# Prescribing TensorE's order in two expert loops, with the scatter and the gather cut in halves

## The chip, the cores and the metric

The kernel runs on one core of one Trainium2 chip. Its time is the device time in microseconds (us) of one launch. TensorE (PE) multiplies matrices and writes to PSUM; VectorE (DVE), ScalarE (ACT) and GpSimd (POOL) do the rest; SyncE (SP) only issues the loads of the weights. Each engine works off its own instructions strictly in the order in which they stand, so an instruction that has to wait holds up all behind it on that engine.

## The reference

Two layers over 256 tokens of 1024 channels, each a mixer and then an expert layer. Layer 0 mixes by attention and a recurrence, layer 1 by a Fourier transform. The expert layer is the same in both: a router picks two of sixteen experts for each token, and each expert is a gated product.

```
h2 = modulate(rmsnorm(x), shift2, scale2)
gates = top-2 of 16 experts per token, inside the best of 4 groups
for e in range(16):
    y = (silu(h2 @ w_gate[e]) * (h2 @ w_up[e])) @ w_down[e]     # 1024 -> 512 -> 1024, float32
    out = out + gates[..., e] * y
x = x + gate2 * out
```

## The kernel before

**Tiling.** Each expert has a list of up to 64 tokens. Two experts make a pair, one in the lower and one in the upper 64 columns of TensorE, and there are 8 pairs (p = 0 to 7) in a layer. Each pair does, in `up` and `down`: 16 matmuls `g` and 16 matmuls `u` (L1045; 8 channel chunks times 2 experts, alternating), the transposes `st` of the pair's one-hot rows (L1054), the activation `act` on ACT and DVE (L1050, L1051), the transposes `at` of `act` (L1064), the copy `aT` on DVE (L1066), and 16 matmuls `dn` in two column halves (L1079), whose results ACT and DVE bring out as `yH` and `yL` (L1081, L1082).

**Around the pairs.** `scatter` (L1018) adds a pair's `yH` and `yL` to the token rows: 8 matmuls `ya` with the one-hot matrix `ST`. It is called one pair later. `gather` (L977) builds the rows of four experts, that is of two pairs: a one-hot matrix `S` on DVE, and 32 matmuls `xg`, brought out of PSUM in eight pieces by ACT and DVE. It is called in the odd pairs 1, 3 and 5 for the two pairs that follow. `st` and `at` share one PSUM bank (`gps`); `g`, `u`, `xg`, `dn` and the final `z` share three (`wps`). Ahead of pair 2 stands `overflow`, a branch that all engines take past code that is not run here; before it `gate_rows` makes two matmuls `gb` (L428) and two copies on ACT (L429).

**The end.** In layer 1 the last pair goes to the output directly: `dn` in four pieces of 256 columns, and after each the four matmuls `z` (L1032) that spread it over the tokens. `up(7)` is called before `down(6)` there.

**The weights.** They run through 16 buffers of 1 MiB in one fixed order (`Stream`, L94); SP issues a load when the buffer's last reader is done. A pair needs 12 MiB.

**What sets the order.** The calls above only give each instruction a place in the program. Which instruction each engine gets next is decided, when the kernel is built, by a scheduler that plays the program through with modelled durations and takes what it believes ready. So instructions of `scatter` and `gather` may end up between those of `g`, `u` and `dn`.

Of the kernel before, what the change touches and what calls it, by code (L numbers as in the profile page):

```python
# [23 lines left out]
# weight buffers, each half a chunk  # L24
NSLOT = 16
# priority of splitting weights, and how far the modulation products stand back
PRI = 50
LOW = 60
# modulation chunks (layer, chunk) in the order they are worked off; those of ON_PE go to the tensor engine
ADA = [(0, 4), (0, 5), (0, 6), (0, 7), (0, 8), (0, 9), (1, 0), (1, 2), (1, 1), (1, 3), (1, 6)]  # L30
ON_PE = (2, 3, 9)
# chunks done in the waits of the expert layers, and beside the Fourier mixer
# [3 lines left out]
# load order of the mixer: modulation chunk (a), attention biases (B), projections Q, G, V, output rows o and p  # L36
ORDER = 'aaQBaaGaaaVpoaaaa'
# engine that takes the low part of each weight piece in K, Q, G, V and the two output products: vector or GpSimd
# [6 lines left out]
# steps of other work put between the steps of a product: modulation, then gates, scan, convolution or attention  # L45
# [6 lines left out]
# columns of the down projection, and of its last pair  # L52
# [4 lines left out]
class Chunk:  # L57
    """A [K * 128, f] piece of weights in two buffers: its first and second rows, or (by_cols) columns."""
# [26 lines left out]
    def used(self, k):  # L85
        """The k-th rows have had their last use."""
        if (k + 1) % self.n == 0:
            self.done(k // self.n)
# [5 lines left out]
class Stream:  # L94
    """Weights run through a fixed set of buffers, loaded in one order as buffers come free."""
# [13 lines left out]
    def add(self, items):  # L109
        """Items: a chunk; (chunk, half) or (chunk, half, columns) for a piece of it; or the (out, in) of another load."""  # L110
        for it in items:
            self.items.extend([(it, 0), (it, 1)] if isinstance(it, Chunk) else [it])
# [34 lines left out]
def hybrid_layers(  # L147
# [73 lines left out]
    def exp_items(l):  # L221
        order = [(n, p) for p in range(NE // 2) for n in "gud"]
        if l == 1:
            order[-6:] = [(n, p) for ns in ("gu", "d") for p in (6, 7) for n in ns]
        r = []
        for n, p in order:
            pair = [st.chunk((n, l, e), {"g": moe_g, "u": moe_u, "d": moe_d}[n][l, e], n == "d")
                    for e in (2 * p, 2 * p + 1)]
            if (l, n, p) == (1, "d", 7):
                # the last weights arrive in small pieces, so that the end of the work keeps up with them  # L230
                r += [(c, a // 512, slice(a % 512, a % 512 + b - a)) for a, b in zip(CUTS, CUTS[1:]) for c in pair]
            else:
                r += [(c, i) for i in range(2) for c in pair]
        return r
# [21 lines left out]
    # the first sections come in pieces, so that the first projection can start on the first channels  # L256
# [65 lines left out]
    def table(f, dep):  # L322
        """Have the activation table of f loaded ahead of its use, once dep is there."""
        return ac.activation(junk, dep, f, scale=0.0, bias=eps)

    def ada_te(l, parts, with_ctx=False, ps_=gps, after=None, used=None):
        """[1024, 128] pieces of the modulation product on the tensor engine; parts: (weights, column, section column).
        Returns the last step, which adds the bias."""
# [30 lines left out]
    def ada_step(l, j):  # L359
        """ada_pe as a task."""  # L360
        while not st.get(("a", l, j)).ready(1):
            yield
        finish = ada_pe(l, j)
        yield
        finish()
        yield

    def ada_ve(l, j):
        """One [1024, 512] piece of the modulation product: scaled rows summed lane by lane, then over the lanes."""
# [22 lines left out]
    def split(dst_h, src, dst_l, eng):  # L392
        """src = dst_h + dst_l exactly, both in float32r's precision."""
# [3 lines left out]
    def split_w(W, eng=gp):  # L397
        """A [128, 512] piece of weights in its two parts."""
# [6 lines left out]
    def mm3(p, lhs, rhs, start, stop):  # L405
        """p += lhs^T rhs from the split operands (high, low)."""
# [4 lines left out]
    def scale_col(name, mod, o, gain, s=slice(0, 8)):  # L411
        """gain * (1 + scale), per channel."""
# [6 lines left out]
    def gate_rows(l, o):  # L419
        """Broadcast a gate section (a column per channel chunk) over all partitions: [128, 1024]."""  # L420
# [11 lines left out]
    def rms_scale(src, dst, tb):  # L432
        """dst[:, tb] = src[:, tb] / rms over the channels."""
# [8 lines left out]
    class Task:  # L442
        """Work emitted step by step between the steps of other work."""
# [43 lines left out]
    # ==== layer 0: mixer ====  # L487
# [30 lines left out]
    def rows(p, w, nt, k):  # L518
        """p[t] += h[tokens of tile t] @ W[chunk k]"""
# [4 lines left out]
    def channels(p, w, n, k):  # L524
        """p[b] += (h[first n tokens] @ W[chunk k])^T, b a block of 128 channels; blocks that share a bank
        make one group, which its first matmul opens and its last one closes."""
# [5 lines left out]
    # x branch of the recurrence, transposed: [channels, latent | context]  # L532
# [19 lines left out]
    # freed buffers: attention biases with the recurrence's gate weights, keys, and queries with the output gate  # L552
# [30 lines left out]
    # depthwise convolution  # L583
# [19 lines left out]
    def gemm(W, step, on):  # L603
        """Eight steps over the contraction, the weights split two steps ahead, on the engines named by on."""
# [16 lines left out]
    def head_norm(ps_, dstT, gain):  # L621
        """QK-norm of [128 tokens, 8 heads x 64] tiles, transposed into dstT."""
# [24 lines left out]
    class Recurrence:  # L647
        """One direction of the gated linear recurrence over [channels, latent | context]."""
# [106 lines left out]
    # neighbourhood + context attention  # L755
# [36 lines left out]
    def weighted(h):  # L792
        """Heads h and h + 1, side by side on the tensor engine."""
# [27 lines left out]
    def add_gated(p, gate, tb, c, eng=ve):  # L821
        """x[columns c] += gate * p"""
# [5 lines left out]
    def project(srcH, srcL, W, order, on):  # L828
        """src^T @ W in four accumulators (token tile, half), src [128, 8, 256] with channels on partitions."""
# [41 lines left out]
    # ==== expert layer ====  # L871
    def normed(p4, gate, into=None):
        """x += gate * mix; returns x over its rms."""
# [8 lines left out]
    def moe(l, xn, store):  # L882
# [19 lines left out]
        # logits: partial sums over the channels in four column groups, added up on the way to token rows  # L902
# [15 lines left out]
        # x over its rms in two exact parts  # L918
# [10 lines left out]
        def place(val, n, name):  # L929
            """How many of the four come before each one, greater first and ties by index: val [128, n, 4]."""  # L930
# [20 lines left out]
        # position of each token in its experts' lists (from 1; 0: not routed), and the lists' lengths  # L951
# [25 lines left out]
        def gather(b):  # L977
            """Experts 4b .. 4b + 3: their tokens' rows, modulated and transposed: [channels, 4 lists of 64]."""
# [6 lines left out]
            for kk in range(4):  # L985
                p = wps("xg")
# [19 lines left out]
            return xg  # L1006
# [4 lines left out]
        yacc = [acc("ya") for _ in range(4)]  # L1011
        at_xg = [None]
        xg = gather(0)
# [4 lines left out]
        def scatter(p, yH, yL, ST):  # L1018
            for tb in range(2):
# [5 lines left out]
        def finish(c, yH, yL, ST):  # L1025
            """The last pair's share of columns c of the output, which are then complete."""
# [10 lines left out]
        def up(p, xg):  # L1037
            """Hidden values of pair p, one expert per half of the partitions, with its one-hot rows and gates."""
# [22 lines left out]
        def down(p, act, gcol, ST):  # L1061
# [4 lines left out]
            ve.tensor_copy(aT, w)  # L1066
            last = store and p == 7
# [23 lines left out]
        for p in range(8):  # L1091
            if p == 2:
                scatter(*pend)
                pend = None
                gate = gate_rows(l, 40)
                overflow(l, ci, over, xh, xl, a2, b2, gate)
            u = early or up(p, xg)
            if p == 0:
                for f in fins:
                    f()  # L1100
            if pend:
                scatter(*pend)
            if p % 2 == 1 and p < 7:
                nxt = gather(p // 2 + 1)
            if p == 5 and l == 0:
                load_dft()
            if store and p == 6:
                early = up(7, xg)
            pend = down(*u)
            if p % 2 == 1 and p < 7:  # L1110
                xg = nxt
        if not store:
            scatter(*pend)
        return yacc, gate

    def overflow(l, ci, over, xh, xl, a2, b2, gate):
        """Tokens past an expert's list: every expert over all tokens, weighted by their gates alone."""
# [39 lines left out]
    def fill(l, n, after=None):  # L1157
        """Modulation pieces to work off in the waits of the expert layer; returns their last steps."""
# [11 lines left out]
    # ==== layer 1: Fourier mixer ====  # L1170
# [6 lines left out]
    # positions: cosine sums for frequencies 0 .. 128 and sine sums for 1 .. 127; the others mirror them  # L1177
# [11 lines left out]
    # channels of a group: frequencies 0 .. 127 from cosine minus sine products, 129 .. 255 (falling) from their sum,  # L1189
    # and 128 in place of the second half's frequency 0  # L1190
# [36 lines left out]
def lay_out(x, c, ctx, c_ctx, ada_w, ada_b, norm_mix, norm_ffn, mix_w_in, mix_w_out, na_q_norm, na_k_norm, na_rpb,  # L1227
# [8 lines left out]
    # weights in the pieces that are loaded at a time: [halves, 128 partitions, rows of a partition, columns]  # L1236
# [3 lines left out]
    # rows of each group in the order of the frequencies on chip: 0 .. 127, then 128, 255, 254, .. 129  # L1240
# [63 lines left out]
```

## Time and profile before

| what | us |
|---|---|
| median of 3 timed runs (831.72 to 833.36) | 832.26 |
| span of the profiled execution | 828.6 |
| TensorE busy in it | 731.2 (88%) |
| expert loop of layer 0, pairs 0 to 7 | 277.2 to 501.7 |
| expert loop of layer 1, to the last matmul | 586.2 to 824.0 |

The page lists the span of the profiled execution, from its first to its last instruction; the timed runs have some 3.7 us more around it. The span is cut into 40 slices of 20.7 us on the page. Times in the trace count from the span's start. Busy time of TensorE is not the measure of what can be saved: a matmul that runs alone in half of the columns is as busy as two that run side by side.

### The profile page before, as it was taken

The numbers are of one execution on the slowest core, as the hardware profiler recorded it, in microseconds if no ns is written. First come the engines' busy times: TensorE is split into PE (matmuls) and PEld (weight loads), VectorE is DVE, ScalarE is ACT, GpSimd is POOL, SyncE is SP. The second block draws the span as 40 slices with busy tenths as digits, with TensorE's granted clock in tenths as the row PEclk, the third lists the DMA queues.
The fourth block names the chain that finished last, engine by engine and source line by source line (L and its number), as shares of the span: only waits on it lengthen the run. The fifth ranks groups of instructions, "written<-read, shape, count | busy, mean of one in ns | idle before, by whom it ended". The sixth has DMA issues, their size and how long they took to land. (4 is left out here: it accounts for less than half of the span.)

```text
span 828.6 us, 10302 instructions
## 1 busy us (share of the span) xinstructions
PE 731.2 (88%) x4048; PEld 393.5 (47%) x4048; DVE 350.2 (42%) x648; ACT 237.8 (29%) x420; POOL 123.4 (15%) x100
## 2 busy tenths in 40 slices
PE   3999869799998899699999996985999699998996
PEld 2676657665556435235434433663535235443333
DVE  4468898897856222012112116857112012112014
ACT  5356748653556101101011004525102001011000
POOL 1131653361112001000000000232001000000001
PEclk8899989887999999899999997997899899999999
DMA  8987458457768899799999999975499799999951
GB/s 281 364 354 281 174 211 318 173 199 299 299 243 310 331 422 421 279 424 421 421 421 421 419 422 421 421 286 240 189 423 420 323 423 420 422 422 421 416 182 51
DMA packets 53788, 277.33 MB, mean 335 GB/s; under 512 B 4898, under 2 KB 20832, under 8 KB 22496
## 3 DMA queue, kind: packets, MB, share of 16 engines
q1 hardware_dynamic: 53584, 276.47, 83.6%
q8 instruction: 36, 0.59, 0.3%
q14 instruction: 24, 0.20, 0.1%
q10 hardware_dynamic: 144, 0.07, 0.0%
HBM read 275.47 MB, written 1.05 MB: 334 GB/s over the span
## 5 line engine op out<-in xcount | busy, mean ns | idle before, releaser
L1045 PE MATMUL g<-slot,xg 128*64 128x512 f32 x512 | 121.8, 613 | 13.0 <-DVEq L1119 13.0
L1079 PE MATMUL dn<-slot,aT 128*64 128x512 f32 (+1 forms) x544 | 121.1, 578 | 11.6 <-DVE aT L1066 4.8
L1045 PE MATMUL u<-slot,xg 128*64 128x512 f32 x512 | 119.2, 593 | 0.0
L1051 DVE TENSOR_TENSOR act<-act,u 128x512 f32<-128x512 f32 x16 | 11.0, 688 | 188.2 <-PE u L1045 164.8
L395 POOL TENSOR_TENSOR wp<-slot,wp 128x512 fp32r<-128x512 f32 x41 | 58.4, 1431 | 157.8 <-ACT wp L394 145.3
L1045 PEld LDWEIGHTS g<-slot,xg 128*64 128x64 f32 x512 | 41.1, 142 | 85.1 <-issue 84.8
L1081 ACT ACTIVATE yH<-dn,gcol 128x512 fp32r<-128x512 f32 (+1 forms) x34 | 22.5, 662 | 204.8 <-PE dn L1079 201.7
L1079 PEld LDWEIGHTS dn<-slot,aT 128*64 128x64 f32 x544 | 41.6, 138 | 76.4 <-issue 63.8
L1045 PEld LDWEIGHTS u<-slot,xg 128*64 128x64 f32 x512 | 40.4, 137 | 69.6 <-issue 67.5
L381 DVE SCALAR_TENSOR_TENSOR gva<-slot,sc,gva 128x512 f32<-128x512 f32 x77 | 72.5, 942 | 1.1
L1082 DVE SCALAR_TENSOR_TENSOR yL<-dn,gcol,yH 128x512 fp32r<-128x512 f32 (+1 forms) x34 | 24.5, 719 | 110.2 <-ACT yH L1081 110.2
L394 ACT ACTIVATE wp<-slot 128x512 fp32r<-128x512 f32 x72 | 44.2, 626 | 48.6 <-PE mix L409 17.9
L1003 POOL TENSOR_TENSOR SG<-S,gates 128x512 f32<-128x512 f32 x8 | 8.4, 1044 | 303.2 <-PE st L1054 208.1
L1050 ACT ACTIVATE act<-g 128x512 f32<-128x512 f32 x16 | 9.6, 597 | 132.6 <-PE g L1045 132.6
L1001 ACT ACTIVATE xg<-xg,modc,a 128x256 f32<-128x256 f32 x32 | 18.1, 565 | 85.3 <-PE xg L992 85.3
L333 PE MATMUL gv<-slot,sc 128*32 128x128 f32 x832 | 34.5, 296 | 7.6 <-DVE modc L350 5.1
L999 DVE TENSOR_SCALAR xg<-xg,a,modc 128x256 f32<-128x256 f32 x32 | 17.4, 543 | 47.3 <-ACT xg L1001 47.3
L333 PEld LDWEIGHTS gv<-slot,sc 128*32 128x32 f32 x832 | 27.8, 119 | 14.8 <-DVE modc L350 5.3
L992 PE MATMUL xg<-S,xh 128*128 128x256 f32 x128 | 28.4, 300 | 3.5 <-DVE S L982 1.7
L395 DVE TENSOR_TENSOR wp<-slot,wp 128x512 fp32r<-128x512 f32 x31 | 24.6, 798 | 8.0 <-ACT wp L394 8.0
L992 PE MATMUL xg<-S,xl 128*128 128x256 f32 x128 | 27.1, 295 | 0.0
L1022 PE MATMUL ya<-yH,ST 128*128 128x512 f32 x60 | 24.1, 421 | 1.9 <-ACT yH L1081 1.9
(258 smaller groups left out, 1127.5 us busy)
## 6 DMA issues: line engine op xcount, KB each, us to landing
slot<-in_moe_g_dram SPq DMA_DIRECT2D x64, 1024.0 KB, 12.6
slot<-in_moe_u_dram SPq DMA_DIRECT2D x64, 1024.0 KB, 13.6
slot<-in_moe_d_dram SPq DMA_DIRECT2D x60, 1024.0 KB, 15.1
slot<-in_ada_w_dram SPq DMA_DIRECT2D x40, 1024.0 KB, 7.2
slot<-in_w_in_dram SPq DMA_DIRECT2D x8, 1024.0 KB, 8.2
slot<-in_ada_w_dram SPq DMA_DIRECT2D x12, 512.0 KB, 9.3
slot<-in_w_out_dram SPq DMA_DIRECT2D x4, 1024.0 KB, 4.9
slot<-in_fnet_w_dram SPq DMA_DIRECT2D x4, 1024.0 KB, 19.8
```

What stands on the lines that cost most here:

```text
L333: te.matmul(out=p[32 * q:32 * q + 32, 0:128], lhsT=sc32[:, k, :], rhs=W[:, k, c:c + 128], start=(k == 0), stop=(k == 7))
L381: ve.scalar_tensor_tensor(r, W[:, k], sc32[:, k, 0:1], r, op0=ALU.mult, op1=ALU.add)
L394: ac.activation(dst_h, src, AF.Copy)
L395: eng.tensor_tensor(dst_l, src, dst_h.bitcast(F32), op=ALU.subtract)
L992: at_xg[0] = te.matmul(out=p[:, i * 256:(i + 1) * 256], lhsT=xx[:, tb, k * 128:(k + 1) * 128], rhs=S[:, tb * 256:(tb + 1) * 256], start=(n ...
L999: ve.tensor_scalar(xg[:, k], pv, a2[:, k:k + 1], b2[:, k:k + 1], op0=ALU.mult, op1=ALU.add)
L1001: ac.activation(xg[:, k], pv, AF.Identity, scale=a2[:, k:k + 1], bias=b2[:, k:k + 1])
L1022: te.matmul(out=yacc[tb * 2 + h], lhsT=ST[:, tb * 128:(tb + 1) * 128], rhs=y[:, h * 512:(h + 1) * 512], start=(p == 0 and n == 0), stop=(n ...
L1045: te.matmul(out=q[half(i), :], lhsT=xg[:, k, half(i0 + i)], rhs=W[i][:, k], start=(k == 0), stop=(k == 7))
L1079: te.matmul(out=dn[half(i), :], lhsT=aT[:, fc * 128 + 64 * i:fc * 128 + 64 * i + 64], rhs=W[i][:, fc, c], start=(fc == 0), stop=(fc == 3))
L1081: ac.activation(yH[:, c], dn, AF.Copy, scale=gcol)
L1082: ve.scalar_tensor_tensor(yL[:, c], dn, gcol, yH[:, c].bitcast(F32), op0=ALU.mult, op1=ALU.subtract)
```

## The change

Inside the pair loop TensorE's order is now the order of the program text (`manual_schedule` for that engine alone); the other engines are still ordered by the scheduler. `gather` becomes a generator that stops after half of its matmuls (16 of 32), and `scatter` may be called for one token tile (4 of 8 matmuls). The transposes and the copy `aT` become a function of their own. The text of the loop puts half a scatter between `st` and `at`, and the other half and half a gather between `at` and `dn`. In pairs 0 and 2, which have no scatter there, the half gather stands ahead of `at`. A gather is therefore begun one pair earlier, in the even pairs 0, 2 and 4, and ended in the odd ones. The other hunks of the diff take away comments.

```diff
         def gather(b):
             ...
             for kk in range(4):
+                if kk == 2:
+                    yield xg
                 p = wps("xg")
             ...
-            return xg
+            yield xg
...
-        def scatter(p, yH, yL, ST):
-            for tb in range(2):
+        def scatter(p, yH, yL, ST, tbs=(0, 1)):
+            for tb in tbs:
...
-        def down(p, act, gcol, ST):
+        def transposed_act(act):
             w = gps("at")
             for q in range(4):
                 te.transpose(w[:, q * 128:(q + 1) * 128], act[:, q * 128:(q + 1) * 128], ident)
             aT = t2k("aT")[:, 0:512]
             ve.tensor_copy(aT, w)
+            return aT
+
+        def down(p, aT, gcol, ST):
...
-        for p in range(8):
-            if p == 2: ...
-            u = early or up(p, xg)
-            ...
-            if pend:
-                scatter(*pend)
-            if p % 2 == 1 and p < 7:
-                nxt = gather(p // 2 + 1)
-            if p == 5 and l == 0:
-                load_dft()
-            if store and p == 6:
-                early = up(7, xg)
-            pend = down(*u)
-            if p % 2 == 1 and p < 7:
-                xg = nxt
+        with tc.manual_schedule(engines={mybir.EngineType.PE}):
+            for p in range(8):
+                if p == 2: ...
+                u = early or up(p, xg)
+                ...
+                ahead = store and p == 6
+                if pend:
+                    scatter(*pend, (0, 1) if ahead else (0,))
+                if p < 6 and p % 2 == 0:
+                    nxt = gather(p // 2 + 1)
+                if p < 6 and not pend:
+                    xg_ = next(nxt)
+                if ahead:
+                    early = up(7, xg)
+                act_t = transposed_act(u[1])
+                if pend and not ahead:
+                    scatter(*pend, (1,))
+                    if p < 6:
+                        xg_ = next(nxt)
+                if p == 5 and l == 0:
+                    load_dft()
+                pend = down(u[0], act_t, *u[2:])
+                if p % 2 == 1 and p < 7:
+                    xg = xg_
```

On TensorE, pair 5 of layer 0 before, where `g` ends and `u` begins (the two `slot` numbers of a product are the two experts' weights):

```order
L1045 MATMUL g<-slot_6263,xg 64x512
L1045 MATMUL g<-slot_6265,xg 64x512
L1022 MATMUL ya<-yL,ST 128x512
L1022 MATMUL ya<-yH,ST 128x512
L1045 MATMUL u<-slot_6277,xg 64x512
L1022 MATMUL ya<-yL,ST 128x512
L1022 MATMUL ya<-yH,ST 128x512
L1022 MATMUL ya<-yL,ST 128x512
```

One matmul of `u` for the first expert stands alone between matmuls of the scatter; its partner for the second expert (slot 6279) comes nine rows later. `g` and `u` of this pair are cut in this way four times.

On TensorE, the same pair 5 now, from the end of `u` on:

```order
L1049 MATMUL u<-slot_6291,xg 64x512
L1058 MATMUL st<-cst,SG 128x128 x2
L1026 MATMUL ya<-yH,ST 128x512
L1026 MATMUL ya<-yL,ST 128x512
L1026 MATMUL ya<-yH,ST 128x512
L1026 MATMUL ya<-yL,ST 128x512
L1068 MATMUL at<-cst,act 128x128 x4
L1026 MATMUL ya<-yH,ST 128x512
L1026 MATMUL ya<-yL,ST 128x512
L1026 MATMUL ya<-yH,ST 128x512
L1026 MATMUL ya<-yL,ST 128x512
L995 MATMUL xg<-S,xh 128x256 x2
```

The two experts' matmuls alternate without a break, and the scatter and half of the gather stand around `at`, in one piece each. `dn` follows after 16 matmuls `xg`.

On TensorE, the last pair's pieces in layer 1, before:

```order
L1079 MATMUL dn<-slot_11450,aT 64x256
L1079 MATMUL dn<-slot_11452,aT 64x256
L1032 MATMUL z<-yH,ST 128x256
L1079 MATMUL dn<-slot_11450,aT 64x256
L1079 MATMUL dn<-slot_11452,aT 64x256
L1079 MATMUL dn<-slot_11450,aT 64x256
L1079 MATMUL dn<-slot_11452,aT 64x256
L1079 MATMUL dn<-slot_11450,aT 64x256
L1032 MATMUL z<-yL,ST 128x256
```

and now:

```order
L1086 MATMUL dn<-slot_11455,aT 64x256
L1086 MATMUL dn<-slot_11457,aT 64x256
L1036 MATMUL z<-yH,ST 128x256
L1036 MATMUL z<-yL,ST 128x256
L1036 MATMUL z<-yH,ST 128x256
L1036 MATMUL z<-yL,ST 128x256
L1086 MATMUL dn<-slot_11455,aT 64x256
```

Before, the next piece of `dn` stood between the four matmuls `z` of the piece in front; now all four `z` come first.

## Rows read from the trace of the kernel before

**Rows 1.** The page's 40 slices: TensorE, its granted clock, DMA share, GB/s.

```profile
PE   3999869799998899699999996985999699998996
PEclk8899989887999999899999997997899899999999
DMA  8987458457768899799999999975499799999951
GB/s 281 364 354 281 174 211 318 173 199 299 299 243 310 331 422 421 279 424 421 421 421 421 419 422 421 421 286 240 189 423 420 323 423 420 422 422 421 416 182 51
```

**Rows 2.** Windows, one pair each: length, TensorE busy (count), clock, DMA share, GB/s.

```profile
277.20:302.83 25.63, 23.57 (x104) 0.93 0.85 351
302.83:331.07 28.24, 27.41 (x144) 1.00 1.01 421
341.75:367.21 25.46, 23.77 (x101) 0.91 0.76 309
367.21:395.27 28.06, 27.23 (x145) 1.00 1.01 421
395.27:419.63 24.36, 23.51 (x112) 1.00 1.01 422
419.63:453.12 33.49, 31.97 (x145) 1.00 1.01 421
477.42:501.65 24.23, 23.45 (x112) 1.00 1.01 421
586.22:610.14 23.92, 21.86 (x103) 1.00 0.81 330
726.81:753.40 26.59, 25.07 (x113) 1.00 1.01 422
```

**Rows 3.** Groups by line: u of pair 4, then u and g of pair 5.

```profile
L1045 PE MATMUL u<-slot,xg 128*64 128x512 f32 x32 | 7.1, 592 | 0.0
...
L1045 PE MATMUL u<-slot,xg 128*64 128x512 f32 x32 | 9.4, 602 | 0.0
L1045 PE MATMUL g<-slot,xg 128*64 128x512 f32 x32 | 8.1, 595 | 0.0
```

**Rows 4.** Timeline, pair 6 of layer 0, TensorE, then DVE: start, length, instruction, [idle before].

```profile
466.98 0.44 PE L1054 MATMUL st<-cst,SG 128*128 128x128 f32 x2
...
469.12 0.60 PE L1064 MATMUL at<-cst,act 128*128 128x128 f32 x4
470.50 1.08 PE L1079 MATMUL dn<-slot,aT 128*64 128x512 f32 x4 [0.78 <-DVE aT L1066]
...
469.75 0.69 DVE L1066 COPY aT<-at 128x512 f32<-128x512 f32 x1 [1.24 <-PE at L1064]
```

**Rows 5.** Timeline of TensorE, pair 0 of layer 0; then a window of it.

```profile
291.09 0.44 PE L1054 MATMUL st<-cst,SG 128*128 128x128 f32 x2
292.80 0.63 PE L1064 MATMUL at<-cst,act 128*128 128x128 f32 x4 [1.27 <-DVE ST L1058]
...
296.00:298.00 2.00, 2.00 (x8) 0.50 1.04 426
```

**Rows 6.** Timeline at the branch of layer 0: ACT, then TensorE.

```profile
334.95 0.60 ACT L429 ACTIVATE gate<-gb 128x512 f32<-128x512 f32 x1 [0.73 <-PE gb L428]
...
341.75 9.35 PE L1045 MATMUL g<-slot,xg 128*64 128x512 f32 x32 [6.62 <-DVEq L1119]
```

**Rows 7.** SP's loads of pair 7's down weights, layer 0; their times from issue to landing.

```profile
464.16 7.78 SPq L130 DMA_DIRECT2D slot<-in_moe_d_dram  x4
...
DMA to landing us min/median/max: 19.8/19.8/19.8
```

**Rows 8.** Timeline of TensorE in layer 1: dn of pair 5, and the end.

```profile
753.40 1.04 PE L1079 MATMUL dn<-slot,aT 128*64 128x512 f32 x2 [0.87 <-issue]
...
820.35 1.94 PE L1079 MATMUL dn<-slot,aT 128*64 128x256 f32 x14
...
823.37 0.39 PE L1032 MATMUL z<-yL,ST 128*128 128x256 f32 x1
```

More of the change, by code (lines that the diff above doesn't have):

```diff
@@ L1012, in moe @@
         at_xg = [None]
-        xg = gather(0)
+        xg = [*gather(0)][-1]
         with tc.issue_after(at_xg[0].ins):
@@ L1090, in moe @@
         early = None
-        for p in range(8):
-            if p == 2:
-                scatter(*pend)
-                pend = None
-                gate = gate_rows(l, 40)
-                overflow(l, ci, over, xh, xl, a2, b2, gate)
-            u = early or up(p, xg)
-            if p == 0:
-                for f in fins:
-                    f()
-            if pend:
-                scatter(*pend)
-            if p % 2 == 1 and p < 7:
-                nxt = gather(p // 2 + 1)
-            if p == 5 and l == 0:
-                load_dft()
-            if store and p == 6:
-                early = up(7, xg)
-            pend = down(*u)
-            if p % 2 == 1 and p < 7:
-                xg = nxt
-        if not store:
-            scatter(*pend)
+        with tc.manual_schedule(engines={mybir.EngineType.PE}):
+            for p in range(8):
+                if p == 2:
+                    scatter(*pend)
+                    pend = None
+                    gate = gate_rows(l, 40)
+                    overflow(l, ci, over, xh, xl, a2, b2, gate)
+                u = early or up(p, xg)
+                if p == 0:
+                    for f in fins:
+                        f()
+                ahead = store and p == 6
[17 more added lines that the diff above has]
+                    xg = xg_
+            if not store:
+                scatter(*pend)
         return yacc, gate
```

## The prediction

> **What bounds the kernel now.** I read the page's 40 slices first. From slice 18 (counted from 1) on the DMA line stands at 9 and GB/s at about 421 almost throughout, which looks like a kernel bound by its weights [rows 1]. The reader is to see that it isn't, in two places: in slices 27 to 29, between the loops, the loads fall to 286, 240 and 189 GB/s because the buffers are full, and the last two slices move 182 and 51 GB/s while TensorE still works [rows 1]. Next I read the waits of TensorE by who ended them: no wait for a weight load is among them in either loop. So the weights come ahead, and TensorE sets the time, with a lead that shrinks: a pair takes 12 MiB, 29.9 us at 421 GB/s, and TensorE needs 24 to 28 us for one [rows 2].
>
> Then one window per pair. Pair 7 takes 24.23 us; pairs 1 and 3, which have a whole gather, 28.24 and 28.06; but pair 5, with the same work as pair 3, takes 33.49 [rows 2]. The groups by line say where: `u` is busy 9.4 us there and 7.1 in pair 4, `g` 8.1 [rows 3]. Two experts' matmuls run side by side in the two halves of the columns (32 records in 7.1 us though one lasts 592 ns). Where the scheduler put scatter and gather in between, pieces of 9, 7, 1, 7, 1 and 7 matmuls are left, all odd, and each odd piece has one that runs alone.
>
> A pair's other losses are two waits: `at` for `act` and for the PSUM bank that `st` used, and `dn` for the copy `aT`.
>
> **The change, step by step.** From `st` to `dn` pair 6 takes 470.50 - 466.98 = 3.52 us [rows 4]. Pair 7, with the same steps, takes 24.23, so the three products cost 20.7 [rows 2]. In pair 6 the eight `ya` fill 2.14 us behind `st`, 0.24 each after 0.2 for `st`; `at` to `dn` is 1.38, in which `aT` hides nothing but `at` itself [rows 4]. A whole gather is 28.24 - 24.36 = 3.9 us (pair 1 less pair 4), a half 1.95.
>
> - *A pair with scatter and half a gather (1, 3, 5).* `at` can't start before `ST` has read the shared bank: 292.80 - 291.09 = 1.71 us after `st` [rows 5]. Four `ya` cover 1.2 of it; 0.5 is a new wait. Then `at` 0.45, four `ya` 0.95, half a gather 1.95: `dn` starts 5.1 after `st`. `aT`, ready 1.38 after `at`, is hidden. The pair costs 25.8: pair 1 saves 2.4, pair 3 2.3, pair 5 33.49 - 25.8 = 7.7.
> - *Pair 4* took 24.36 and gets half a gather: 25.8. On DVE the new `S` now stands behind `aT`; it is an operation of the size of `aT`, 0.69 us, so the gather waits some 0.6 for it. Pair 4 loses 2.0.
> - *Pair 2* has its half gather ahead of `at`, 2.15 after `st`, and then the 1.38 to `dn` uncovered: 3.55. Its 25.46 contain a `g` of 9.35 after the branch for the usual 7.1 [rows 2, 3, 6]; that stays. 20.7 + 2.3 + 3.55 = 26.6, a loss of 1.1.
> - *Pair 0* likewise comes to 24.3. In layer 0 it took 25.63, because after two waits TensorE's granted clock fell to 0.50, that is 1.2 GHz [rows 2, 5]; in layer 1, with the same waits, it didn't, and the pair took 23.92, 1.7 less [rows 2]. The longer wait (1.27) goes. I take the clock as kept: -1.3 and +0.4; if it falls, 1.7 more.
> - *Pairs 6 and 7 of layer 0*: 1.71 + 0.45 + 0.95 = 3.1 for 3.52, each -0.4.
> - *The branch.* Before, two `yL` matmuls were put behind `gb`; now all eight `ya` stand ahead, and the second half of pair 1's `yH` and `yL` is waited for. I put that at 0.8 us, since ACT's last copy (334.95) ended just before the 6.62 us stall and now ends later [rows 6]. Bounds: 0, and 1.5 (two evictions like `aT`).
>
> Layer 0: -1.3 - 2.4 + 0.8 + 1.1 - 2.3 + 2.0 - 7.7 - 0.4 - 0.4 = -10.6. But here the lead of the weights is used up. Pair 7's last down piece is issued at 471.6 and lands 19.8 later, at 491.4, and the pieces land 2.49 us apart (1 MiB at 421 GB/s), so its last `u` piece lands at 481.4 [rows 7]. That time hangs on the branch alone, behind which the loads begin anew. TensorE, 7.3 us further than before since the branch, would want that piece, half a `u` into pair 7 (477.42 + 6.9 + 3.45 = 487.8 before), at 480.5. It waits 0.9: layer 0 gives **-9.7**.
>
> The Fourier mixer between the loops I cost at nothing: it moves earlier as a whole, and its own loads, which follow the experts' in the queue, are used many microseconds after they land. Bounds: -1 (TensorE's order there changes a little) and +4 (late loads).
>
> Layer 1 up to `dn` of pair 5, with layer 0's terms taken over: +0.4 - 2.4 + 0.8 + 1.1 - 2.3 + 2.0, and for pair 5 up to `dn` 26.59 - (13.8 + 5.1) = 7.7 saved: -8.1 [rows 2]. From there to the last `dn`'s end it took 822.29 - 753.40 = 68.9 [rows 8]. Now: `dn`, `g`, `u` 20.7; `st` and eight `ya` 2.1; `g` and `u` of pair 7 13.8; `st` to `at` 1.7 (the shared bank, a new wait of 1.3); `at` to `dn` 1.4; `dn` 6.9; half a scatter that waits for the last `yH` and `yL` (two operations like `aT`, with their hand-overs), 2.0; `at` and the other half 1.45; four pieces of `dn`, 1.72 each, 6.9; and between them three times `z`. The row prices that: from the last `dn`'s end (822.29) to the first `z` with `yL` (823.37) it took 1.08, so with the rest of `z` 1.6 per piece, 4.8, and 0.3 for DVE, which has four `gm` in front [rows 8]. Sum 62.1: -6.8. Weights are not late here: loads end in slice 39, which begins at 787 and moves 182 GB/s, some 10 us before its last pieces are used [rows 1]. Layer 1 gives **-14.9**.
>
> Sum -24.6. One new pair of waits (`at` 1.3, `dn` 0.8 in pair 7's stead) has the shape after which the clock fell in one layer and not in the other: half of 1.7. Rounded for small losses at the changes of form, **-23**: span 828.6 - 23 = 805.6; with the 3.7 us by which the median of the timed runs, 832.3, exceeds it, **809.5 us**.
>
> A rule of the Trainium skill bears on the forms: "TensorEngine Tiling (Array Packing)", Key Properties, says that changing the tiling mode drains TensorE. Pair 5 had about eight such changes more than pair 3 and cost 5.4 us more [rows 2]; by the lone halves alone it would be six times 0.43, 2.6. So part of the loss may be drains, and both go with the cuts; by the rule the halved scatter and gather cost nothing new, since each pair keeps two changes.
>
> **The rivals.**
> *Weights take over.* In layer 0 the lead ends in pair 7; were it to end sooner, as with a landing rate a few per cent lower or a later restart behind the branch, TensorE would run at 29.9 us a pair. For it speaks the margin of nothing in layer 0, against it that layer 1 starts with full buffers. Price 5 us in layer 0, 3 in layer 1: 817.5.
> *The clock.* TensorE falls to 1.2 GHz after waits, at 1.7 us [rows 5] to 2.3 [rows 6] a time. The new 0.5 at each `at` could bring four more falls: +8, 817.5. Against it: at the end of layer 1 TensorE is busy 6 and 9 tenths, and the last two slices still show a clock of 9 [rows 1].
> The Trainium skill, "TensorE: Matmul & The Clock Gate", What's actually happening, calls the throttled state the default, which activity releases; by that the fuller loop is safer, and the trace, with 1.00 in all unbroken pairs, agrees [rows 2].
> *The mixer eats it.* Layer 0's 9.7 are lost if DVE's modulation products in the mixer wait for their own weights, whose landing times hardly move: 819. Against it: they lay landed for some 9 us before.
> *Slower.* With a prescribed order one late operand stops all behind it. The place is `at`: if on DVE a gather's eviction or `S` stood ahead of `act`, `ST` or `aT` in most pairs, each of 16 pairs would lose a vector operation and its wait. It decides from 23/16 = 1.45 us a pair on; at 1.7 the time is 836. Against it: `aT` stands ahead of the evictions wherever TensorE reaches `dn` soon.
>
> **How the numbers follow.** The forecast has 0.58, with a range of its own of 806 to 814; weights 0.15; clock 0.12; mixer 0.09; slower, or a change that nets nothing, 0.06. The range of 804 to 820 leaves out the slower case and a few per cent at either end. A difference under 0.2%, 1.7 us, can't be told from none: faster 0.94, same 0.01, slower 0.05.
>
> **What would show it.** Right: `u` and `g` 7.1 us in all pairs, pair 5 at about 25.8, `dn` waiting for `aT` only in pairs 0, 2 and 6 of layer 1, a wait of 0.5 before most `at`, and TensorE's first wait for a load at the end of layer 0. Wrong: pairs 1 to 5 above 27, waits for loads in several pairs, half clock inside unbroken pairs, or the mixer longer by several us.

## The result, and the profile after

The changed kernel takes 806.59 us (median of 4 runs, 803.68 to 807.31), the one before 832.81 in the same comparison: ratio 0.9687, 95% interval 0.9664 to 0.9711. Forecast were 809.5, 804 to 820. The profiled execution is the fastest of the four, 803.68, with a span of 801.9: 26.7 less than before, where 23 were forecast. A run's time is thus some 1.8 us above its own span, not 3.7: the execution profiled before, 828.6 + 1.8 = 830.4 by this estimate, was also faster than its kernel's median.

The page of the kernel after, TensorE, its granted clock, DMA share and GB/s in 40 slices:

```profile
PE   3999869898999899799999996978699799999986
PEclk9999998896999999999999999999899999999999
DMA  8987477564768899999999999999199999999991
GB/s 275 358 340 288 172 262 264 212 261 159 300 261 313 338 370 422 417 403 423 419 423 419 422 419 421 423 416 355 63 424 422 402 423 423 420 422 420 422 375 63
```

Against [rows 1], the loads now run at 400 and more from slice 16 to slice 27 without a gap, and the clock stands at 9 in every slice that lies inside a loop (short falls, as behind the branches, can hide in a 9).

One window per pair, layer 0 and the first of layer 1 (length, TensorE busy with its count, clock, DMA share, GB/s):

```profile
278.02:302.31 24.29, 23.50 (x120) 1.00 0.86 351
302.31:331.07 28.76, 27.98 (x136) 1.00 1.01 419
337.21:363.19 25.98, 25.14 (x118) 0.94 0.99 407
363.19:389.04 25.85, 25.53 (x129) 1.00 1.01 421
389.04:415.62 26.58, 25.79 (x129) 1.00 1.01 421
415.62:441.46 25.84, 25.50 (x129) 1.00 1.01 421
441.46:465.68 24.22, 23.61 (x113) 1.00 1.01 420
465.68:490.20 24.52, 24.20 (x113) 1.00 1.01 421
574.52:598.85 24.33, 23.55 (x119) 1.00 0.81 331
```

Pair 5 takes 25.84 instead of 33.49, with the busy time gone that its lone matmuls had taken, and with half a gather for its whole one; pair 4 pays 2.2 for its half gather, pair 2 0.5 [rows 2]. The second window reaches to pair 1's scatter of eight `ya`, which stands ahead of the branch; up to the end of `dn` pair 1 takes about 25.8.

The waits of TensorE by who ended them (total, times, longest):

```profile
PE g L1049 <- PEq L1137: 7.9, 2, 4.2
PE at L1068 <- DVE ST L1062: 4.3, 10, 1.2
PE dn L1086 <- DVE aT L1070: 4.1, 5, 0.9
PE xg L995 <- DVE S L983: 2.6, 3, 1.7
PE z L1036 <- ACT yH L1088: 2.4, 4, 0.6
```

The first row is the two branches; the others are the waits that the forecast named, except that the longest wait for `S`, 1.7, lies ahead of a loop and is the same before. No wait for expert weights is listed; one too short to be listed shows in `u` of pair 7 of layer 0 (below).

### The profile page after: what moved, and what is told of

Its sections match the earlier page's. It is cut to its first block, busy times and chain, and to the rows that moved or that the text cites. A ratio compares the mean times of both kernels' runs of the same rounds, so it can differ in the third digit from the quotient of the medians.

```text
span 801.9 us, 10308 instructions
## 1 busy us (share of the span) xinstructions
PE 716.3 (89%) x4048; PEld 383.0 (48%) x4048; DVE 351.6 (44%) x648; ACT 237.8 (30%) x420; POOL 124.8 (16%) x100
## 5 line engine op out<-in xcount | busy, mean ns | idle before, releaser
L1049 PE MATMUL g<-slot,xg 128*64 128x512 f32 x512 | 116.1, 607 | 7.9 <-PEq L1137 7.9
L1086 PE MATMUL dn<-slot,aT 128*64 128x512 f32 (+1 forms) x544 | 115.6, 577 | 4.1 <-DVE aT L1070 4.1
L1049 PE MATMUL u<-slot,xg 128*64 128x512 f32 x512 | 113.1, 592 | 0.0
L1049 PEld LDWEIGHTS g<-slot,xg 128*64 128x64 f32 x512 | 37.9, 140 | 82.1 <-issue 81.3
L1049 PEld LDWEIGHTS u<-slot,xg 128*64 128x64 f32 x512 | 38.0, 137 | 72.4 <-issue 71.8
L1086 PEld LDWEIGHTS dn<-slot,aT 128*64 128x64 f32 x544 | 37.8, 138 | 70.6 <-issue 61.0
L1026 PE MATMUL ya<-yH,ST 128*128 128x512 f32 x60 | 26.3, 439 | 0.6 <-ACT yH L1088 0.5
L995 PE MATMUL xg<-S,xl 128*128 128x256 f32 x128 | 26.4, 288 | 0.0
```

The source lines that it names most:

```text
L995: at_xg[0] = te.matmul(out=p[:, i * 256:(i + 1) * 256], lhsT=xx[:, tb, k * 128:(k + 1) * 128], rhs=S[:, tb * 256:(tb + 1) * 256], start=(n ...
L1026: te.matmul(out=yacc[tb * 2 + h], lhsT=ST[:, tb * 128:(tb + 1) * 128], rhs=y[:, h * 512:(h + 1) * 512], start=(p == 0 and n == 0), stop=(n ...
L1049: te.matmul(out=q[half(i), :], lhsT=xg[:, k, half(i0 + i)], rhs=W[i][:, k], start=(k == 0), stop=(k == 7))
L1086: te.matmul(out=dn[half(i), :], lhsT=aT[:, fc * 128 + 64 * i:fc * 128 + 64 * i + 64], rhs=W[i][:, fc, c], start=(fc == 0), stop=(fc == 3))
```

## The experiments

Stretches are read from the profiled executions: "loop" is the time from the first `g` of a layer to the end of its last `dn`. Before, it was 224.7 in layer 0 and 236.1 in layer 1; after, 212.3 and 221.1. What lies ahead of the loops differs from run to run by up to 5 us (the first `g` starts between 277.2 and 282.5), so loops are compared, not spans.

**The order alone.** The kernel before, its text unchanged, with TensorE's order prescribed:

```diff
-        for p in range(8):
-            ...
+        with tc.manual_schedule(engines={mybir.EngineType.PE}):
+            for p in range(8):
+                ...
```

> TensorE's order is prescribed as the old text has it: scatter whole between st and at, gather whole behind it in the odd pairs, no halves. My theory (the gain comes first from the column pairs that are no longer cut into odd pieces, in pair 5 of both layers and at the end of layer 1, and only then from the halves that cover waits): u and g take 7.1 us in every pair, pair 5 falls from 33.5 to 28.2 us, pairs 0 to 4 stay as they were, layer 0 gains 5 to 6, layer 1 some 5 to 8 with its end, and the two branches 1.7 each, since no st and gcol stand ahead of them: 815 us, 812 to 819. Rival 1 (the halves carry the gain): 824 to 830. Rival 2 (the order is all of it): 805 to 809.

Measured: 814.96, ratio 0.9789 (0.9773 to 0.9805). The loops take 216.3 and 225.9, pair 5 28.7 and 28.1. So of 25.9 us the order alone brings 17.5, two thirds, and the halves on top of it 8.4. Theory held, both rivals fell. Not all of it is lone halves: of the 18.6 us that the two loops gained, pair 5 brings 4.8 in layer 0 and 5.4 in layer 1 (up to `dn`), the end of layer 1 3.1, and the two branches 3.5, since `st` and `gcol` now stand behind them. 1.7 is luck: in pair 0 of layer 0 the clock didn't fall this time, behind the same two waits.

**The halves alone.** The changed text, with the scheduler ordering TensorE:

```diff
-        with tc.manual_schedule(engines={mybir.EngineType.PE}):
+        if True:
             for p in range(8):
```

> The text of the changed kernel, with halves, but the scheduler orders TensorE as before. It cuts even more column pairs: by count some 12 odd pieces in the expert loop of layer 0 (pairs 5 to 7) and some 24 in that of layer 1 (pairs 1, 5, 6, 7 and the end), where the changed kernel has none. My theory: each odd piece costs 0.43 us for its lone matmul and something for the change of form, 15 us or more, of which layer 0 gives none to the covered waits: 820 to 828 us, with u of pair 1 in layer 1 at 9 us or more. Rival (the halves carry the gain, the order is beside the point): 805 to 810. The branch: in layer 0 st stands ahead of it (wait of g behind it 6 us or more, as before the change), in layer 1 not (4 us, as after), if gcol on DVE is what delays it; if not, both are alike.

Measured: 839.61, ratio 1.0081 (1.0053 to 1.0108): slower than before. Without the order the halves do harm. Timeline of TensorE, pair 1 of layer 1 (start, length, instruction, count):

```profile
630.19 1.07 PE L1049 MATMUL u<-slot,xg 128*64 128x512 f32 x2
631.19 0.50 PE L1026 MATMUL ya<-yL,ST 128*128 128x512 f32 x1
...
633.16 0.40 PE L995 MATMUL xg<-S,xl 128*128 128x256 f32 x2
633.49 3.65 PE L1049 MATMUL u<-slot,xg 128*64 128x512 f32 x14
```

More and smaller blocks give the scheduler more places to cut: here one `u` matmul (two records) stands alone, then seven. I had it slower than the changed kernel, as it is, but still faster than the one before, and was 12 to 20 us short: beside lone halves and changes of form (below), this order has waits of `ya` for `yH`, 5.9, and of `at` for `act`, 5.0, which before the change are 1.9 and 4.1 and after it 0.5 and 0.6. The expectation on the branch fell too: in layer 1 no `st` stands ahead of it, and `g` still waited 6.7.

**What a cut costs.** In ten pairs, the first half scatter moved into the middle of `u`: behind its 8th matmul, or behind its 7th.

```diff
                     for i in range(2):
                         te.matmul(out=q[half(i), :], ..., start=(k == 0), stop=(k == 7))
+                        if between and n == "u" and (k, i) == (3, 1):    # odd: (3, 0)
+                            between()                                    # scatter(*pend, (0,))
```

> The changed kernel, but in ten pairs (1 and 3 to 7 of layer 0, 1 and 3 to 5 of layer 1) the first half scatter stands in the middle of u, between its 8th and 9th matmul: two even pieces, no lone matmul. It measures what a change of form alone costs. Theory (the lone halves were the larger part of what the cuts cost; st between dn and g cost 0.3 us in the run with st ahead of g): u lasts 7.04 + 0.95 of the four ya + 0.3; and at waits 1.25 instead of 0.3 to 0.5 since its cover is gone, so 1.2 a pair: 817 to 820 us, more by 1.7 for each clock that falls after that wait. Rival (the change of form is the cost): u lasts 8.9 or more, 824 us or more.

> The same as the even cut, but between the 7th and the 8th matmul of u: pieces of 7 and 9, each with one matmul that runs alone in half of the columns. Theory (a lone matmul costs 0.43 us): u longer by 0.86 than with the even cut, in ten pairs, so 8.6 us slower than it. Rival (a cut costs the same wherever it stands; the change of form is the cost): no more than 1 us slower.

Measured: even 817.92, odd 828.25. Timeline of TensorE, pair 4 of layer 0, even cut:

```profile
399.99 3.60 PE L1049 MATMUL u<-slot,xg 128*64 128x512 f32 x16
403.53 0.50 PE L1026 MATMUL ya<-yH,ST 128*128 128x512 f32 x1
...
404.65 3.65 PE L1049 MATMUL u<-slot,xg 128*64 128x512 f32 x16
408.24 0.44 PE L1060 MATMUL st<-cst,SG 128*128 128x128 f32 x2
409.95 0.63 PE L1070 MATMUL at<-cst,act 128*128 128x128 f32 x4 [1.27 <-DVE ST L1064]
```

and the same pair with the odd cut:

```profile
405.83 3.60 PE L1049 MATMUL u<-slot,xg 128*64 128x512 f32 x14
409.36 0.50 PE L1026 MATMUL ya<-yH,ST 128*128 128x512 f32 x1
...
410.49 4.51 PE L1049 MATMUL u<-slot,xg 128*64 128x512 f32 x18
414.92 0.44 PE L1060 MATMUL st<-cst,SG 128*128 128x128 f32 x2
```

and in the changed kernel, uncut:

```profile
395.90 7.04 PE L1049 MATMUL u<-slot,xg 128*64 128x512 f32 x32
402.87 0.44 PE L1058 MATMUL st<-cst,SG 128*128 128x128 f32 x2
```

From `u`'s start to `st` it takes 408.24 - 399.99 = 8.25 with the even cut and 9.09 with the odd one. Uncut it is 6.97, and four `ya` are 0.95. So a change of form and back costs 8.25 - 7.92 = 0.33, and each lone matmul 0.84 / 2 = 0.42. The seven-matmul piece takes as long as the eight-matmul one, 3.5 us: the half that is missing is not saved. Ten pairs give 8.4 of the 12.0 by which the loops of the two profiled executions differ (10.3 between the medians); the rest is the clock: in the odd run `g` of pair 2 is 1.1 longer in each layer and `dn` of pair 6 in layer 1 1.7 longer. Both theories held; the rival, that a cut costs the same wherever it stands, fell.

**The branch.** In the changed kernel, `st` and `gcol` of pair 2 put ahead of the branch again:

```diff
                     gate = gate_rows(l, 40)
+                    pre = rows_of(2)                 # st, gcol
                     overflow(l, ci, over, xh, xl, a2, b2, gate)
-                u = early or up(p, xg)
+                u = early or up(p, xg, pre if p == 2 else None)
```

> The changed kernel, but st and gcol of pair 2 stand ahead of the branch again, as in the kernel before, in both layers. Theory (DVE comes late to the branch because gcol waits there for TensorE's last product, and g behind the branch waits for DVE): the wait of g behind the branch grows from 4.2 and 3.8 us to over 6, +2 each, less 0.5 for the st that no longer stands in pair 2: 809 to 811 us. Rival (the branch became shorter for another reason: the scatter in front of it, loads or code that come at other times): waits of 3.8 to 4.4, 805.5 to 807.5 us.

Measured: 810.72, 4.1 more than the changed kernel; `g` waits 12.7 us in the two branches instead of 7.9. VectorE at the branch of layer 0 (start, length, [idle before]), first in the kernel before:

```profile
331.91 0.75 DVE L1082 SCALAR_TENSOR_TENSOR yL<-dn,gcol,yH 128x512 fp32r<-128x512 f32 x1 [2.68 <-ACT yH L1081]
335.17 0.42 DVE L1056 TENSOR_REDUCE gcol<-st 128x1 f32<-128x256 f32 x1 [2.51 <-PE st L1054]
341.66 0.42 DVE L1058 TENSOR_SCALAR ST<-st 128x256 fp32r<-128x256 f32 x1 [6.07 <-DVEq L1119]
```

then in the kernel after:

```profile
329.10 0.75 DVE L1089 SCALAR_TENSOR_TENSOR yL<-dn,gcol,yH 128x512 fp32r<-128x512 f32 x1 [2.68 <-ACT yH L1088]
336.87 0.69 DVE L983 TENSOR_TENSOR S<-cst,rank 128x512 fp32r<-128x512 f32 x1 [7.01 <-PEq L1137]
```

Between `yL` and the first instruction behind the branch there were 9.0 us, now 7.0: `gcol` had waited 2.5 for `st`, which stood last on TensorE, and the trip past the skipped code began only then. VectorE with `st` and `gcol` put ahead again:

```profile
333.14 0.42 DVE L1047 TENSOR_REDUCE gcol<-st 128x1 f32<-128x256 f32 x1 [3.45 <-PE st L1045]
339.46 0.42 DVE L1067 TENSOR_SCALAR ST<-st 128x256 fp32r<-128x256 f32 x1 [5.90 <-DVEq L1143]
```

In this run the other two engines end their work ahead of the branch when they do in the kernel after, TensorE at 333.10 for 333.06 and ACT at 333.52 for 333.69. Only VectorE ends later, 333.56 for 329.85, and the first instruction behind the branch comes 2.6 us later. That rules out ACT and TensorE as the cause of the difference. The halves alone, layer 1, tell TensorE's own way apart once more. TensorE there:

```profile
653.70 0.72 PE L1026 MATMUL ya<-yL,ST 128*128 128x512 f32 x2
661.13 4.53 PE L1049 MATMUL g<-slot,xg 128*64 128x512 f32 x10 [6.71 <-PEq L1137]
```

and VectorE:

```profile
652.89 0.75 DVE L1089 SCALAR_TENSOR_TENSOR yL<-dn,gcol,yH 128x512 fp32r<-128x512 f32 x1 [6.84 <-ACT yH L1088]
660.90 0.42 DVE L1062 TENSOR_SCALAR ST<-st 128x256 fp32r<-128x256 f32 x1 [7.26 <-PEq L1137]
```

No `st` is ahead of the branch, TensorE waits 6.7 us all the same, and VectorE the usual 7.3 after its `yL`. In the nine kernels in which VectorE's first instruction behind the branch waits for no other engine, both layers, it came 6.7 to 7.3 us after `yL` or 5.6 to 6.1 after `gcol`, and TensorE's wait varied from 3.5 to 6.7 with the time by which its own work ended before that. So VectorE's arrival sets the length. What it does in that time, and why it is a microsecond less after `gcol`, no row shows.

**`st` ahead of `g`.** The changed kernel with `st`, `gcol` and `ST` of a pair ahead of its `g`:

```diff
         def up(p, xg):
+            gcol, ST = rows_of(p)                    # st, gcol, ST: no longer behind u
             gu = [wps("g"), wps("u")]
```

> The changed kernel with st, gcol and ST of each pair ahead of its g instead of behind its u. at then no longer waits for ST in the shared bank (4.3 us in 10 waits), only for act, which is there some 0.9 us after u; four ya cover it. Theory: 0.4 us a pair, ten pairs, but in pairs 3 to 7 of layer 0 the weights set the time, so some 1.5 of it turns into waits for loads at pair 7: 802 to 804.5 us, no at<-ST among the waits. Rival 1 (act takes ST's place in the wait): no gain, 806 to 808. Rival 2 (weights don't bind in layer 0): 801 to 802.5.

Measured: 804.52, ratio 0.9669 (0.9653 to 0.9686); against 0.9687 the intervals overlap, so a gain of 2 us isn't shown by the times. In the trace the ten waits of `at` for `ST` are gone, but pairs 3 and 5 gain 0.2 only: `st` now stands between `dn` and `g` and brings its own change of form, the 0.33. In layer 0 nothing came of it: `g` behind the branch ran 0.8 longer, at a lower clock, and in pair 7 `u` grew to 8.0 and `dn` to 7.5, which fits weights that came no earlier. Layer 1 is 3.3 shorter, 2.6 of it at the end, more than half by the clock (below).

**All waits covered.** `st` behind the last product of the pair before, `S` ahead of `g`, the half gather of pairs 0 and 2 as two quarters around `at`, and at the end of layer 1 `at` of pair 6 ahead of pair 7's `g` and each `z` one piece of `dn` later:

```diff
+                if p < 6 and p % 2 == 0:
+                    nxt = gather(p // 2 + 1)
+                    next(nxt)                        # S alone
                 ...
+                elif p < 6:
+                    next(nxt)                        # a quarter, ahead of at
                 aT = transposed_act(act)
                 ...
+                if p != 1 and p < 7:
+                    R[p + 1] = rows_of(p + 1)        # st, gcol, ST
                 if store and p == 6:
+                    act = up(7, xg)[1]
+                    pend = down(6, aT, *R[6])
+                    aT = transposed_act(act)
                     ...
```

> The changed kernel with its remaining waits covered: st stands in the pair before, behind the last product there (for pairs 0 and 2 ahead of g), S ahead of g in the even pairs, the half gather of pairs 0 and 2 as two quarters around at, in layer 1 at of pair 6 ahead of pair 7's g, and each z one piece of dn later. Theory (weights set the time of layer 0 from the branch on, TensorE that of layer 1): layer 0 gains 1.5 before the branch and nothing behind it, its u of pair 7 grows to 9 to 11 us by waits for loads; layer 1 gains 3 in its pairs and 8 to 9 from pair 6 to the end: 794 us, 790 to 798. Rival (weights don't bind, layer 0 gains its 4 as well): 790 to 792. Rival (the waits were covered by nothing that counts, or weights bind in layer 1 too): 799 to 805.

Measured: 798.17, ratio 0.9616 (0.9573 to 0.9660): the fastest of all, its four runs (796.67 to 802.59) all below the changed kernel's. The time is 4 us above the forecast and just outside its range, and its parts are not as forecast: layer 0 gained nothing at all (212.0), layer 1 8.1, of which 6 in pairs 0 to 5 and 2 at the end, and not 3 and 9. 1.7 of the 6 is the clock: `g` behind the branch took 7.09 for 8.79. Timeline of TensorE, pair 7 of layer 0 and then of layer 1:

```profile
468.65 3.22 PE L1059 MATMUL g<-slot,xg 128*64 128x512 f32 x13 [1.31 <-DMA slot<-in_moe_g_dram]
...
473.62 3.65 PE L1059 MATMUL u<-slot,xg 128*64 128x512 f32 x16 [1.32 <-DMA slot<-in_moe_u_dram]
478.60 3.65 PE L1059 MATMUL u<-slot,xg 128*64 128x512 f32 x14 [1.32 <-DMA slot<-in_moe_u_dram]
...
762.54 4.92 PE L1059 MATMUL u<-slot,xg 128*64 128x512 f32 x13 [2.32 <-DMA slot<-in_moe_u_dram]
...
772.57 3.65 PE L1090 MATMUL dn<-slot,aT 128*64 128x512 f32 x14 [1.24 <-DMA slot<-in_moe_d_dram]
```

Here the weights have taken over, in both layers. So the theory, which had TensorE set the time of layer 1, failed there, and the second rival had the mechanism, though not the time.

**Fewer weights.** To show that these waits are the weights, `d` of pair 4 isn't loaded, and its products use `u`'s buffers; once with all waits covered, once in the changed kernel:

```diff
-                r += [(c, i) for i in range(2) for c in pair]
+                r += [(c, i) for i in range(2) for c in pair if (n, p) != ("d", 4)]
...
-            W = [st.get(("d", l, 2 * p + i)) for i in range(2)]
+            W = [st.get(("u" if p == 4 else "d", l, 2 * p + i)) for i in range(2)]
```

> The kernel with all waits covered (measured 798.2), but d of pair 4 is not loaded in either layer: its products take the buffers of u of that pair, which are kept until then (so these products are computed with other numbers). 4 MiB less come in each layer, 10 us of loading at 421 GB/s; TensorE's work is the same. Theory (in that kernel the weights set the time): all waits of g, u and dn for loads go, 4.4 us in layer 0 and 3.6 in layer 1: 790 us, 788 to 793. Rival (the waits put down to loads are something else, or what is left is TensorE's own): 796 to 799.

> The changed kernel itself, with d of pair 4 not loaded in either layer, in the same way (these products are computed with other numbers). Theory (here TensorE still sets the time in both loops, and the weights are only just in time in pair 7 of layer 0, whose u is 0.5 us long): 0.5 to 1 us faster, 805 to 807. Rival (weights have already taken over in the changed kernel): 4 us or more faster, 803 or less.

Measured: 789.46 with all waits covered (8.7 less, loops 207.5 and 209.1, no wait for expert weights), and 807.62 in the changed kernel, no different from its 806.59 (loops 212.7 and 221.2). In the first, `g` behind the branches took 9.9 and 9.6 us for 8.2 and 7.1, at a lower clock (0.71 and 0.74 for 0.86 and 1.00), so the weights cost more than the 8.7. In the second, `u` of pair 7 of layer 0 is back at full speed:

```profile
476.30 7.04 PE L1049 MATMUL u<-slot,xg 128*64 128x512 f32 x32
```

It took 7.54 in the changed kernel, so that 0.5 was weights, as forecast; the loop is no shorter, since `g` behind its branch took 9.4 for 8.6. In the changed kernel TensorE sets the time and the weights are just in time; 8 us further on it is the weights.

## Why the prediction was right, and where it wasn't

**The mechanism** was right: the lone halves. Pair 5 had six odd pieces and five changes of form and back more than pair 3 (ten single changes, where the forecast counted about eight): 6 x 0.42 + 5 x 0.33 = 4.2 of the 5.4 us by which it was longer. The rest wasn't taken apart. The forecast had left open whether drains are part of it; the changes of form are, with 1.7 of it. The Trainium skill, "TensorEngine Tiling (Array Packing)", Key Properties, has TensorE drained when the tiling mode changes; the trace agrees in that a change costs time, 0.33 for the way there and back, though no row shows the drain itself. The larger part, the half array that stands idle, is not in that rule.

**Pairs** (forecast, then measured, layer 0): pair 0 24.3, 24.29; pair 1 25.8, 25.8; pair 2 26.6, 25.98; pair 3 25.8, 25.85; pair 4 26.4, 26.58; pair 5 25.8, 25.84; pair 6 23.9, 24.22. Pair 2's 0.6 less is its `g`, 8.63 for 9.35. Pair 4's `xg` waited for `S` as named, 0.45 us for 0.6:

```profile
406.59 0.50 PE L995 MATMUL xg<-S,xh 128*128 128x256 f32 x2 [0.45 <-DVE S L983]
```

Pair 6 has the wait of `at` for `act` (0.6): on VectorE `gcol` and `ST` stood ahead of `act`, close to what the slower rival had as its mechanism; it happened once. Pair 0's clock stayed at full speed, 1.00 for 0.93, as chosen. The mixer moved as a whole: 84.4 before, 84.3 after.

**The step that failed is the branch**: +0.8 forecast, 10.7 -> 9.1 us measured from the end of `dn` to `g` in layer 0 and 10.4 -> 8.7 in layer 1, so -1.6 and -1.7. I had taken ACT's copy, which ended just before the 6.6 us stall [rows 6], for the latest arrival, and reckoned that it would now end later. It was VectorE's `gcol`, which ended 0.04 later and which the change moves behind the branch. The row that ends just before a stall is not the row that causes it; the prediction didn't look at the third engine. With that, layer 0 gave 12.4 for 9.7 and layer 1 up to pair 5's `dn` 10.9 for 8.1.

**The weights** at the end of layer 0: a wait of 0.9 forecast [rows 7], `u` of pair 7 7.54 for 7.04 measured, so 0.5. That the loads stop at the branch and begin anew behind it was the state of before:

```profile
330.00:340.00 10.00, 5.13 (x20) 0.98 1.02 419
340.00:350.00 10.00, 8.25 (x28) 0.68 0.37 130
```

In the two windows of the kernel before (clock, DMA share, GB/s) they stop; in those of the kernel after they hardly do:

```profile
330.00:340.00 10.00, 5.84 (x17) 0.85 1.01 413
340.00:350.00 10.00, 10.00 (x50) 0.98 0.96 383
```

With `st` and `gcol` ahead again, and the branch 2.3 us longer for it, the second window moves 265 GB/s for 383. So it fits that the shorter branch lets buffers come free about when the queue runs dry.

**The end of layer 1** was mis-sized: from pair 5's `dn` on 6.8 forecast, 4.1 measured (68.9 [rows 8], now 795.58 - 730.83 = 64.75). Timeline of TensorE after:

```profile
769.38 0.63 PE L1068 MATMUL at<-cst,act 128*128 128x128 f32 x4 [1.25 <-DVE ST L1062]
770.86 8.56 PE L1086 MATMUL dn<-slot,aT 128*64 128x512 f32 x32 [0.85 <-DVE aT L1070]
...
782.80 1.95 PE L1086 MATMUL dn<-slot,aT 128*64 128x256 f32 x16
785.37 0.38 PE L1036 MATMUL z<-yH,ST 128*128 128x256 f32 x1 [0.62 <-ACT yH L1088]
...
786.44 1.95 PE L1086 MATMUL dn<-slot,aT 128*64 128x256 f32 x16
```

The new pair of waits was sized right (1.25 and 0.85 for 1.3 and 0.8), and the clock fell behind it: `dn` took 8.56, not 7.09, where I had put half of 1.7. That is 1.5 of the 2.7 us. Each of the pieces takes 786.44 - 782.80 = 3.64 with its `z`, for 3.3 forecast, so three of them are 1.0 more.

**The rivals.** Weights: 0.5 us in the changed kernel, the bound as soon as 8 us more are saved. Inside the pairs the clock fell once, at the place named, not at the new waits of 0.5. The mixer took nothing back. Slower: not with the order, but the halves without it, by 7.2.

**What the total hides.** The branch went the other way from its term (-4.9 over both layers), the end saved 2.7 less than its term, and the first `g` started 0.8 later. The 23 for 26.7 is thus closer than its parts. 1.4 of the saving is luck: `g` behind the two branches took 8.6 and 8.8 us for 9.4 and 9.5, and in the other kernels 7.1 to 9.9, behind short and long waits alike. Of the 2.9 us between the forecast time and the median, 3.7 is the larger saving, less 1.0 because the median lies 4.7 above this span and not 3.7; the rest is rounding. That 1.0 isn't the kernel: the execution profiled after lies 2.9 below its median, the one before some 1.9. Between the medians the saving is 26.2.

## What to carry to other kernels

Two matmuls that share the array in column halves are best taken as one unit: other work is to stand between two such pairs, at an even place, and not within one. The scheduler of this kernel cut at odd places too, and more often with finer blocks. So prescribe the order first and halve the blocks second; the other way round this kernel became slower. At a point that all engines pass, look for the engine that arrives last over its own way, not for the row that ends last; and before covering further waits, work out when the weights bind, since here some 8 us were left until they did.

## What the runs showed of the hardware

- A matmul alone in half of the columns costs as if its partner ran beside it, 0.42 us more than its share of a pair; a change from half-column to full-width matmuls and back costs 0.33.
- Inside the pairs the clock fell behind two waits in a row, 1.2 to 1.6 us before `at` and 0.8 before `dn`, but not each time (besides, once behind a wait of 2.3 us for a load, with all waits covered): in the kernel before in one of two such places, with the order alone in one of five. At the end of layer 1, with the same waits of 1.25 and 0.85, it fell in the changed kernel and in three of the runs made from it (`st` ahead of the branch, odd cut, fewer weights), but not in the one with the even cut, where `dn` took 7.09. A single wait of 1.2 to 1.5 before `at`, with full-width products behind it, came 20 times in the two runs with cuts, and `dn` took 7.09 each time. With `st` ahead of `g` the 1.25 was gone, the 0.87 stayed, and `dn` of pair 6 took 7.09. What decides it in a given place no run shows.
- Past the skipped code of the branch VectorE took 6.7 to 7.3 us after `yL`, and 5.6 to 6.1 after `gcol`, while TensorE waited anything from 3.5 to 6.7.
